# First expert block of 80 slots instead of 128, and two blocks behind branches instead of one

## The chip, the cores and the metric

The kernel runs on one core of a Trainium2 chip. A core has TensorE (PE) for matrix products, VectorE (DVE), ScalarE (ACT), GpSimd (POOL) and SyncE (SP, which issues the loads here); the engines run side by side and wait for each other by semaphores. The metric is the device time of one execution in microseconds; lower is better.

## What is computed

Two layers of a decoder on 256 tokens of width 1024, all in float32. Layer 0 ends in a dense feed-forward block, layer 1 in eight experts, of which each token uses the two with the highest router values:

```python
logits = jnp.dot(x2d, w_router)                    # (256, 8)
top_logits, top_e = lax.top_k(logits, TOP_K)       # two experts of each token
top_w = jax.nn.softmax(top_logits, axis=-1)
...
def expert_block(args):                            # rows of one expert, 1024 wide
    xb, e = args
    return (jax.nn.silu(xb @ w_gate[e]) * (xb @ w_up[e])) @ w_down[e]   # 1024 -> 3584 -> 1024
```

Each token's two results are added, weighted with `top_w`. 512 pairs of token and expert fall on eight experts, 64 on average; with the inputs of the reference the experts get 55, 69, 69, 67, 52, 63, 68 and 69 tokens.

## The kernel before, in words

Everything is written out by hand: no loop is left in the program, and the order on ScalarE and VectorE in the experts is the order of the code (`in_order`). Products are made in three passes of the type float32r: each operand x is split into a rounded part (`xh`) and the rest (`xl`), and `wh.xh + wl.xh + wh.xl` stands for `w.x`. The split of the weights is done by `split` (lines 101 and 102): ScalarE casts a half chunk of 128 x 1024, VectorE subtracts.

The stage of the experts (`moe`, `experts(0)`) goes like this:

- **Routing** (`moe_route`) finds for each token its place among the tokens of its expert (`pos`). `slots` holds the numbers 0 to 127 in every row.
- **Dispatch** (`dispatch`, for two experts at a time) makes a one-hot matrix `oh` of tokens by slots (line 1515), and 32 products (line 1529) gather the tokens of both experts: stationary is a 128-column slice of the tokens `uth` or `utl`, moving is `oh` with 2 x 128 columns. Result: `xh` and `xl`, 1024 on the partitions and slots along the free side. Four transposes of `oh` (line 1535) make `ot`, with which results are sent back.
- **Gate and up** (lines 1638 to 1640): for each expert and each of 7 parts of 512 hidden columns, 2 x 24 products. Stationary are 128 slots of `xh` or `xl`, moving are 512 columns of weights. `hidden` (lines 1252, 1253) makes silu(gate) x up, a tile of slots x 512.
- **Turn** (`turn`, line 1658): four transposes put the 512 hidden columns on the partitions (stationary 128 columns of `hid`, moving the identity), and ScalarE and VectorE split the result into `hh` and `hl` (lines 1661, 1662). It is issued `TURN` = 2 half chunks after `hidden`.
- **Down** (lines 1625 to 1627): 24 products with `hh` and `hl` as stationary and 512 moving weight columns, into two sums of slots x 512 that run over all 7 parts.
- **Bring** (`bring`, `add`, lines 1671 to 1680): the sums are split and sent back to the tokens by eight products with `ot`, and added to `h` with their weights.

Each expert's weights are 42 chunks of 1 MB. SP issues a load when the buffer before it has been read for the last time, which is by VectorE in line 102. TensorE's queue holds, for each expert, 7 x 72 products with 512 moving columns; between them lie the turns, the dispatch of the next pair of experts, and the way back.

Behind the stage stands a branch. `most` is the largest number of tokens of any expert; each engine loads it (line 1504) and jumps (line 1505) over a second copy of the whole block, for slots 128 to 255, which is not run with these inputs. Behind the jump the last stage begins (`ple`: transposes of `h` in line 150, products in lines 271 to 273, the output).

Of the kernel before, what the change touches and what calls it, by code (L numbers as in the profile page):

```python
# [10 lines left out]
F32 = mybir.dt.float32  # L11
F32R = mybir.dt.float32r
# [7 lines left out]
D = 1024  # L20
# [20 lines left out]

RATE = [[[0.9, 0.6, 1.04], [0.31, 0.22, 0.66], [0.3, 0.23, 0.38, 0.3, 0.3], [0.39, 0.25, 0.08, 0.12, 0.29], [2.4, 2.8, 2.8, 2.7], [1.4, 1.0, 0.8, 0.6], [1.0, 1.0, 1.0, 1.0, 1.0, 1.0], [0.0, 1.0, 1.0, 1.0]], [[0.55, 0.85, 1.15], [0.18, 0.12, 0.47], [0.3, 0.3, 0.3, 0.45, 0.3], [0.41, 0.71, 0.1, 0.0, 0.5], [2.7, 2.7, 2.7, 2.7], [0.5, 0.5, 0.5, 0.5], [1.0, 1.0, 1.0, 1.0, 1.0, 1.0], [0.0, 1.0, 1.0, 1.0]]]

LATE = 1
FROM = [6, 8]
WARM = 14, 8, 6
# [25 lines left out]
class Build:  # L72
# [363 lines left out]
    def mixer(self, l):  # L436
# [59 lines left out]
        def zchunks(a, b):  # L496
# [16 lines left out]
            for i, (c, fi) in enumerate(items):  # L513
# [8 lines left out]
                late.append((c, fi, ps))  # L522
                if len(late) > LATE:
                    finish(*late.pop(0))
# [720 lines left out]
                    finish(*late.pop(0))  # L1245
                yield

    def hidden(self, pg, pu, shape):

        nc = self.nc  # L1250
        hid = self.fx.tile(shape, F32, name="hid", tag="hid", bufs=2)
        nc.scalar.activation(hid, pg, AF.Silu)
        nc.vector.tensor_tensor(hid, pu, hid, op=OP.mult)
        return hid
# [245 lines left out]
    def moe(self):  # L1500
        nc, tc = self.nc, self.tc
        self.experts(0)
        if self.general:
            most = nc.values_load(self.cnti[0:1, 0:1], min_val=0, max_val=256)
            with tc.If(most > 128):
                self.experts(1)
        self.tap("hf1", self.h)

    def dispatch(self, e0, blk):

        nc, fx, M = self.nc, self.fx, self.M
        oh = fx.tile([128, 2, 256], F32R, name="oh", tag="oh", bufs=2)
        for tt in range(2):
            for i in range(2):
                nc.vector.tensor_scalar(oh[:, tt, i * 128:(i + 1) * 128], M["slots"], float(128 * blk),
                                        M["pos"][:, tt, e0 + i:e0 + i + 1], op0=OP.add, op1=OP.is_equal)
        yield
        xh = fx.tile([128, 8, 256], F32R, name="xh", tag="xh", bufs=2)
        xl = fx.tile([128, 8, 256], F32R, name="xl", tag="xl", bufs=2)
        ot = fx.tile([128, 2, 2, 128], F32R, name="ot", tag="ot", bufs=2)  # L1520
        self.X[e0 // 2] = xh, xl, ot
        sums = cycle([self.psm] if e0 else [self.psm, self.psz])
        for kp in range(4):
            for src, dst in ((M["uth"], xh), (M["utl"], xl)):
                ps = next(sums)(2, 256)
                for ki in range(2):
                    k = 2 * kp + ki
                    for tt in range(2):
                        nc.tensor.matmul(ps[:, ki], src[:, tt, k * 128:(k + 1) * 128], oh[:, tt], start=tt == 0, stop=tt == 1)
                nc.scalar.copy(dst[:, 2 * kp:2 * kp + 2], ps)  # L1530
                yield
        ps = self.psm(2, 2, 128)
        for i in range(2):
            for tt in range(2):
                nc.tensor.transpose(ps[:, i, tt], oh[:, tt, i * 128:(i + 1) * 128].bitcast(F32), self.ident)
        nc.scalar.copy(ot, ps)
        yield

    def halves(self):
# [21 lines left out]
    def experts(self, blk):  # L1561


        nc, A, fx = self.nc, self.A, self.fx
        mm = nc.tensor.matmul
        X, HID, HT, ACC, PS = self.X, {}, {}, {}, {}
        block = nc.cur_bb.bb

# [45 lines left out]
        def products(j):  # L1614
            w, e, n, i = halves[j]
            wh, wl = splits[j]
            splits[j] = None
            if w == "down":
                hh, hl = HT[e, n]
                if n == 0 and i == 0:  # L1620
                    ACC[e] = [self.psz(512) for _ in range(2)]
                for hf in range(2):
                    ws = slice(hf * 512, (hf + 1) * 512)
                    ps, f, z = ACC[e][hf], n == 0 and i == 0, n == 6 and i == 3
                    mm(ps, hh[:, i], wh[:, ws], start=f, stop=False)  # L1625
                    mm(ps, hh[:, i], wl[:, ws], start=False, stop=False)  # L1626
                    mm(ps, hl[:, i], wh[:, ws], start=False, stop=z)  # L1627
                if n == 6 and i == 3:
                    after(j, 0, lambda: bring(e))
                return  # L1630
            xh, xl, _ = X[e // 2]
            sl = slice((e % 2) * 128, (e % 2) * 128 + 128)
            if i == 0:
                PS[w] = self.psa(512)
            ps = PS[w]
            for ki in range(2):
                k, ws = 2 * i + ki, slice(ki * 512, (ki + 1) * 512)
                mm(ps, xh[:, k, sl], wh[:, ws], start=k == 0, stop=False)  # L1638
                mm(ps, xh[:, k, sl], wl[:, ws], start=False, stop=False)  # L1639
                mm(ps, xl[:, k, sl], wh[:, ws], start=False, stop=k == 7)  # L1640
            if w == "up" and i == 3:
                g, u = PS["gate"], PS["up"]
                after(j, 0, lambda: HID.update({(e, n): self.hidden(g, u, [128, 512])}))
                after(j, TURN, lambda: turn(e, n))
                if e % 2 and n == 1 and e < NE - 1:
                    st = self.dispatch(e + 1, blk)
                    for t in range(10):
                        after(j, 1 + t, lambda: next(st))

        def after(j, lag, fn):  # L1650
            due[j + lag].append(fn)

        def turn(e, n):

            hid = HID.pop((e, n))
            pt = self.psm(4, 128)
            for i in range(4):
                nc.tensor.transpose(pt[:, i], hid[:, i * 128:(i + 1) * 128], self.ident)
            hh = fx.tile([128, 4, 128], F32R, name="hh", tag="hh", bufs=2)
            hl = fx.tile([128, 4, 128], F32R, name="hl", tag="hl", bufs=2)  # L1660
            nc.scalar.copy(hh, pt)
            nc.vector.tensor_sub(hl, pt, hh.bitcast(F32))
            HT[e, n] = hh, hl

        def bring(e):

            acc, ot = ACC.pop(e), X[e // 2][2]
            yh, yl = (lambda t: (t[:, 0], t[:, 1]))(self.fy.tile([128, 2, D], F32R, name="yhl", tag="yhl"))
            for hf in range(2):
                ws = slice(hf * 512, (hf + 1) * 512)  # L1670
                nc.scalar.copy(yh[:, ws], acc[hf])
                nc.vector.tensor_sub(yl[:, ws], acc[hf], yh[:, ws].bitcast(F32))

            def add(tt, hf):
                ws = slice(hf * 512, (hf + 1) * 512)
                ps = self.psm(512)
                mm(ps, ot[:, e % 2, tt], yh[:, ws], start=True, stop=False)
                mm(ps, ot[:, e % 2, tt], yl[:, ws], start=False, stop=True)
# [15 lines left out]
        for j in range(len(due)):  # L1694
            at = j

            for _ in range((4, 2, 2, 0, 1)[j] if j < 5 else 0):
                next(st0)
            if j < len(halves):
                products(j)  # L1700
                split()
                if blk == 0 and j == EMBED - 24:
                    st = embed()
                    after(j, 0, lambda: next(st))
                    for t in range(7):
                        after(j, 24 - LEAD + t, lambda: next(st))
            for fn in due[j]:
                fn()
# [123 lines left out]
```

## Time and profile before

| | us |
|---|---|
| median of 3 runs | 1978.77 (1977.77 to 1978.91) |
| profiled execution | 1978.85 |
| its span, first to last instruction | 1977.1 |
| experts, first dispatch product to the last result added | 954 to 1942 |
| the last stage behind the branch | 1945 to 1977 |

TensorE is busy for 1926.7 us of the span (97%), VectorE for 1589.3 (80%), ScalarE for 1387.2 (70%). Products are pipelined: a record of TensorE runs from its start to a modelled end, so a record of 0.39 us may be followed by the next start after 0.23. What a product costs in a full queue is the distance of starts, and this is what is read below. In the rows a form such as `128*128 128x512` is the stationary operand (rows x columns) and the moving one. PEld is the load of the stationary operand, which overlaps with products. An engine's name with a q (PEldq, SPq) stands for its sequencer: jumps, semaphores, DMA issues.

### The profile page before, as it was taken

How to read it: one execution, taken by the hardware profiler on the slowest of the kernel's cores; microseconds unless marked ns; L12 is line 12 of the kernel's file. 1: busy time of each engine (PE TensorE's matmuls, PEld its weight loads, DVE VectorE, ACT ScalarE, POOL GpSimd, SP SyncE). 2: the span in 40 equal slices, each digit the busy share in tenths (PEclk: the TensorE clock that was granted, in tenths of full speed). 3: DMA queues.
4: the chain of work that ended last, by engine and by line, in shares of the span. 5: the costliest groups of instructions: out<-in, count | busy, mean ns of one | idle time of the engine just before them, and what ended most of it. 6: DMA issues, size and time to landing. Idle time of an engine off the chain costs nothing. (4 is left out here: it accounts for less than half of the span.)

```text
span 1977.1 us, 32507 instructions
## 1 busy us (share of the span) xinstructions
PE 1926.7 (97%) x12357; PEld 1640.6 (83%) x12357; DVE 1589.3 (80%) x2072; ACT 1387.2 (70%) x1981; POOL 13.8 (1%) x50
## 2 busy tenths in 40 slices
PE   8999999999999999999999999999999999999997
PEld 8878789899989868788888888888788888888886
DVE  6879757655576889466899899989899989999995
ACT  6776775644456686574787787878777777777773
POOL 1000000000000000000000000000000000000000
PEclk8999999999999999899999999999999999999999
DMA  5433225555534324048797899999899999999990
GB/s 208 138 115 129 87 103 191 194 191 189 186 129 157 114 97 152 24 155 313 266 365 299 328 373 362 373 368 350 315 361 377 374 333 368 357 383 372 357 360 29
DMA packets 92516, 491.38 MB, mean 249 GB/s; under 512 B 11168, under 2 KB 11424, under 8 KB 53184
## 3 DMA queue, kind: packets, MB, share of 16 engines
q1 hardware_dynamic: 89712, 485.04, 66.4%
q10 hardware_dynamic: 2640, 4.18, 0.7%
q8 instruction: 99, 1.62, 0.3%
q14 instruction: 65, 0.53, 0.1%
HBM read 488.13 MB, written 1.05 MB: 247 GB/s over the span
## 5 line engine op out<-in xcount | busy, mean ns | idle before, releaser
L102 DVE TENSOR_TENSOR wl<-rawm,wh 128x1024 fp32r<-128x1024 f32 x608 | 724.0, 1221 | 65.1 <-ACT wh L101 26.1
L101 ACT CAST wh<-rawm 128x1024 fp32r<-128x1024 f32 x608 | 628.9, 1054 | 117.2 <-PE ps_a L1640 72.8
L102 DVE TENSOR_TENSOR wl<-raw,wh 128x1024 fp32r<-128x1024 f32 x298 | 362.7, 1221 | 158.3 <-PE ps_z L109 89.3
L101 ACT CAST wh<-raw 128x1024 fp32r<-128x1024 f32 x298 | 312.3, 1050 | 132.1 <-PE ps_z L110 35.3
L108 PE MATMUL ps_z<-uh,wh 128*128 128x256 f32 x1232 | 358.9, 291 | 4.3 <-ACT wh L101 2.3
L110 PE MATMUL ps_z<-uh,wl 128*128 128x256 f32 x1232 | 352.3, 286 | 7.3 <-DVE wl L102 7.3
L109 PE MATMUL ps_z<-ul,wh 128*128 128x256 f32 x1232 | 350.1, 284 | 0.0
L1640 PE MATMUL ps_a<-wh,xl 128*128 128x512 f32 x896 | 349.8, 390 | 0.0
L1639 PE MATMUL ps_a<-wl,xh 128*128 128x512 f32 x896 | 349.5, 390 | 0.3 <-DVE wl L102 0.2
L1638 PE MATMUL ps_a<-wh,xh 128*128 128x512 f32 x896 | 349.5, 391 | 0.2 <-ACT wh L101 0.2
L108 PEld LDWEIGHTS ps_z<-uh,wh 128*128 128x128 f32 x1232 | 235.2, 191 | 16.2 <-issue 6.5
L110 PEld LDWEIGHTS ps_z<-uh,wl 128*128 128x128 f32 x1232 | 235.3, 191 | 14.7 <-DVE wl L102 10.7
L109 PEld LDWEIGHTS ps_z<-ul,wh 128*128 128x128 f32 x1232 | 235.2, 191 | 5.8 <-issue 4.4
L1639 PEld LDWEIGHTS ps_a<-wl,xh 128*128 128x128 f32 x896 | 168.3, 188 | 37.6 <-DVE wl L102 1.9
L1638 PEld LDWEIGHTS ps_a<-wh,xh 128*128 128x128 f32 x896 | 168.3, 188 | 35.8 <-ACT wh L101 0.9
L1640 PEld LDWEIGHTS ps_a<-wh,xl 128*128 128x128 f32 x896 | 168.2, 188 | 34.9 <-issue 0.5
L1627 PE MATMUL ps_z<-wh,hl 128*128 128x512 f32 x448 | 176.8, 395 | 0.0
L1626 PE MATMUL ps_z<-wl,hh 128*128 128x512 f32 x448 | 175.2, 391 | 0.4 <-DVE wl L102 0.4
L1625 PE MATMUL ps_z<-wh,hh 128*128 128x512 f32 x448 | 162.6, 397 | 0.2 <-ACT wh L101 0.2
L1626 PEld LDWEIGHTS ps_z<-wl,hh 128*128 128x128 f32 x448 | 84.2, 188 | 18.4 <-DVE wl L102 1.9
L1627 PEld LDWEIGHTS ps_z<-wh,hl 128*128 128x128 f32 x448 | 84.1, 188 | 17.2
L1625 PEld LDWEIGHTS ps_z<-wh,hh 128*128 128x128 f32 x448 | 84.2, 188 | 16.2 <-ACT wh L101 0.6
(556 smaller groups left out, 2433.2 us busy)
## 6 DMA issues: line engine op xcount, KB each, us to landing
rawm<-in_wmg_dram SPq DMA_DIRECT2D x199, 1024.0 KB, 6.6
rawm<-in_wmd_dram SPq DMA_DIRECT2D x101, 1024.0 KB, 6.7
raw<-in_wz_dram SPq DMA_DIRECT2D x112, 512.0 KB, 3.8
raw<-in_wmg_dram SPq DMA_DIRECT2D x50, 512.0 KB, 7.8
raw<-in_wff_dram SPq DMA_DIRECT2D x44, 512.0 KB, 4.1
raw<-in_wbr_dram SPq DMA_DIRECT2D x24, 512.0 KB, 4.7
raw<-in_wfd_dram SPq DMA_DIRECT2D x22, 512.0 KB, 3.7
raw<-in_wmd_dram SPq DMA_DIRECT2D x22, 512.0 KB, 8.0
```

Source lines behind the costliest of these rows:

```text
L101: nc.scalar.copy(h, raw)
L102: nc.vector.tensor_sub(l, raw, h.bitcast(F32))
L108: nc.tensor.matmul(ps, wh, xh, start=first, stop=False)
L109: nc.tensor.matmul(ps, wh, xl, start=False, stop=False)
L110: nc.tensor.matmul(ps, wl, xh, start=False, stop=last)
L1625: mm(ps, hh[:, i], wh[:, ws], start=f, stop=False)
L1626: mm(ps, hh[:, i], wl[:, ws], start=False, stop=False)
L1627: mm(ps, hl[:, i], wh[:, ws], start=False, stop=z)
L1638: mm(ps, xh[:, k, sl], wh[:, ws], start=k == 0, stop=False)
L1639: mm(ps, xh[:, k, sl], wl[:, ws], start=False, stop=False)
L1640: mm(ps, xl[:, k, sl], wh[:, ws], start=False, stop=k == 7)
```

## The change

The slots of an expert are covered by three blocks of 80, 128 and 48 slots instead of two of 128. The first is always run. The other two stand behind branches of their own, at more than 80 and at more than 208 tokens of the fullest expert; a branch follows the end of the other, they are not nested.

In the block every tile keeps its size and is used in part. `oh` has 2 x 80 columns, so the 32 products of a dispatch move 160 columns. `xh` and `xl` get an axis for the expert. The stationary operands of gate, up and down have 80 columns, sums and `hid` 80 partitions, and `turn` multiplies with an 80 x 80 corner of the identity.

```diff
+BLOCKS = ((0, 80), (80, 128), (208, 48))
...
-            with tc.If(most > 128):
-                self.experts(1)
+            for blk in range(1, len(BLOCKS)):
+                with tc.If(most > BLOCKS[blk][0]):
+                    self.experts(blk)
...
-        oh = fx.tile([128, 2, 256], F32R, name="oh", tag="oh", bufs=2)
+        start, cap = BLOCKS[blk]
+        oh = fx.tile([128, 2, 256], F32R, name="oh", tag="oh", bufs=2)[:, :, 0:2 * cap]
...
-                nc.vector.tensor_scalar(oh[:, tt, i * 128:(i + 1) * 128], M["slots"], float(128 * blk),
+                nc.vector.tensor_scalar(oh[:, tt, i * cap:(i + 1) * cap], M["slots"][:, 0:cap], float(start),
...
-        xh = fx.tile([128, 8, 256], F32R, name="xh", tag="xh", bufs=2)
+        xh = fx.tile([128, 8, 2, 128], F32R, name="xh", tag="xh", bufs=2)[:, :, :, 0:cap]
...
-                ps = next(sums)(2, 256)
+                ps = next(sums)(2, 2 * cap)
...
-                nc.scalar.copy(dst[:, 2 * kp:2 * kp + 2], ps)
+                nc.scalar.copy(dst[:, 2 * kp:2 * kp + 2], ps.rearrange("p k (e s) -> p k e s", e=2))
...
-                nc.tensor.transpose(ps[:, i, tt], oh[:, tt, i * 128:(i + 1) * 128].bitcast(F32), self.ident)
-        nc.scalar.copy(ot, ps)
+                nc.tensor.transpose(ps[0:cap, i, tt], oh[:, tt, i * cap:(i + 1) * cap].bitcast(F32), self.ident)
+        nc.scalar.copy(ot[0:cap], ps[0:cap])
...
-                    ACC[e] = [self.psz(512) for _ in range(2)]
+                    ACC[e] = [self.psz(512)[0:cap] for _ in range(2)]
...
-                mm(ps, xh[:, k, sl], wh[:, ws], start=k == 0, stop=False)
+                mm(ps, xh[:, k, e % 2], wh[:, ws], start=k == 0, stop=False)
...
-            pt = self.psm(4, 128)
+            pt = self.psm(4, cap)
             for i in range(4):
-                nc.tensor.transpose(pt[:, i], hid[:, i * 128:(i + 1) * 128], self.ident)
-            hh = fx.tile([128, 4, 128], F32R, name="hh", tag="hh", bufs=2)
+                nc.tensor.transpose(pt[:, i], hid[:, i * 128:(i + 1) * 128], self.ident[0:cap, 0:cap])
+            hh = fx.tile([128, 4, 128], F32R, name="hh", tag="hh", bufs=2)[:, :, 0:cap]
...
-                mm(ps, ot[:, e % 2, tt], yh[:, ws], start=True, stop=False)
+                mm(ps, ot[0:cap, e % 2, tt], yh[:, ws], start=True, stop=False)
```

The program has the same instructions in the part that is run, in nearly the same order. On TensorE, at the start of the block, the order before has the five small products of the routing, six that only keep the engine at work (line 145), and the first dispatch, whose last number is the shape of the result:

```order
L1468 MATMUL ps_m<-msel,onr 128x8
L145 MATMUL ps_z<-ones 128x128 x6
L1529 MATMUL ps_m<-oh,uth 128x256
L1529 MATMUL ps_z<-oh,utl 128x256 x2
L1529 MATMUL ps_m<-oh,uth 128x256 x3
L1529 MATMUL ps_z<-oh,utl 128x256 x6
```

The same place of the change:

```order
L1533 MATMUL ps_m<-oh,uth 128x160
L1533 MATMUL ps_z<-oh,utl 128x160
L1533 MATMUL ps_m<-oh,uth 128x160 x3
L1533 MATMUL ps_z<-oh,utl 128x160 x5
L1533 MATMUL ps_m<-oh,uth 128x160 x4
```

The results have 160 columns instead of 256, and one product of the second sum has moved behind three of the first.

On TensorE at the end of the block, with the last result sent back, the load of `cnti` (the largest count), the jump, the first rows of the block that it passes over, and behind the dots what follows that block, before:

```order
L1678 MATMUL ps_m<-yhl,ot 128x512
L1504 TENSOR_LOAD cnti
L1505 COMPARE_AND_BRANCH
L1529 MATMUL ps_m<-oh,uth 128x256 x4
...
L1505 UNCONDITIONAL_BRANCH x2
L150 MATMUL ps_m<-ident,h 128x128 x8
```

And in the change:

```order
L1682 MATMUL ps_m<-yhl,ot 128x512
L1506 TENSOR_LOAD cnti
L1508 COMPARE_AND_BRANCH
L1533 MATMUL ps_m<-oh,uth 128x256 x4
...
L1508 UNCONDITIONAL_BRANCH x2
L1508 COMPARE_AND_BRANCH
L1533 MATMUL ps_m<-oh,uth 128x96 x4
...
L1508 UNCONDITIONAL_BRANCH x2
L152 MATMUL ps_m<-ident,h 128x128 x8
```

The end of the first passed block is now followed by a second jump over a second block of as many rows, with 2 x 48 columns in its dispatches, and only then by the transposes of the last stage.

## Rows read from the trace of the kernel before

**Rows 1.** Busy time of each engine in the experts' stage, granted clock, DMA.

```profile
core 0: us, PE busy (x) PEld busy (x) DVE busy (x) ACT busy (x) POOL busy (x), PEclk, DMA share, GB/s
1000.00:1900.00 900.00, 899.14 (x4088) 739.87 (x4087) 822.91 (x787) 707.02 (x773) 0.00 (x0) 1.00 0.94 357
```

**Rows 2.** Waits from 1000 to 1900 us (total, times, longest), VectorE for loads.

```profile
DVE wl L102 <- DMA rawm<-in_wmg_dram: 2.0, 3, 1.4
```

**Rows 3.** Waits of SyncE's DMA queue in the same stretch.

```profile
SPq L88 <- DVE wl L102: 725.0, 270, 6.3
```

**Rows 4.** TensorE in order of time, experts: start us, us, line, form.

```profile
1079.43 0.39 PE L1639 MATMUL ps_a<-wl,xh 128*128 128x512 f32 x1
...
1080.80 0.39 PE L1639 MATMUL ps_a<-wl,xh 128*128 128x512 f32 x1
```

**Rows 5.** TensorE in order of time, layer 1's mixer: 128, then 64 stationary columns.

```profile
635.39 0.28 PE L108 MATMUL ps_z<-uh,wh 128*128 128x256 f32 x1
...
636.10 0.28 PE L108 MATMUL ps_m<-uh,k2a 128*64 128x256 f32 x1
...
636.93 0.28 PE L109 MATMUL ps_m<-ul,k2a 128*64 128x256 f32 x1
```

**Rows 6.** TensorE in order of time, layer 1's output projection.

```profile
929.89 0.40 PE L273 MATMUL ps_a<-wh,ul 128*128 128x512 f32 x1
...
931.29 0.40 PE L273 MATMUL ps_a<-wh,ul 128*128 128x512 f32 x1
```

**Rows 7.** TensorE in order of time around one turn.

```profile
1085.10 0.39 PE L1627 MATMUL ps_z<-wh,hl 128*128 128x512 f32 x1
1085.33 0.60 PE L1658 MATMUL ps_m<-ident,hid 128*128 128x128 f32 x4
...
1086.00 0.40 PE L1626 MATMUL ps_z<-wl,hh 128*128 128x512 f32 x1
```

**Rows 8.** Three lines with plain f32: duration ns min/median/max, first and last start.

```profile
L1155 PE MATMUL ps_m<-cv x32: 377/379/634, 202.3 to 845.3; 96*128 96x256 f32 x32
...
L1658 PE MATMUL ps_m<-ident,hid x224: 270/272/273, 973.9 to 1929.5; 128*128 128x128 f32 x112
...
L695 PE MATMUL ps_m<-ident,t x48: 216/222/273, 84.1 to 696.3; 64*128 64x64 f32 x48
```

**Rows 9.** TensorE in order of time in the first dispatch.

```profile
959.99 0.64 PE L1529 MATMUL ps_m<-oh,uth 128*128 128x256 f32 x4
...
960.94 0.40 PE L1638 MATMUL ps_a<-wh,xh 128*128 128x512 f32 x1
```

**Rows 10.** TensorE in order of time in the routing.

```profile
951.96 0.24 PE L1464 MATMUL ps_m<-msel,ltr 128*128 128x8 f32 x1 [0.25 <-ACT wh L101]
...
952.40 0.25 PE L1468 MATMUL ps_m<-msel,onr 128*128 128x8 f32 x1
```

**Rows 11.** Groups of ScalarE by form: busy us, mean ns, idle before.

```profile
L1252 ACT ACTIVATE hid<-ps_a 128x512 f32<-128x512 f32 x56 | 33.0, 589 | 0.0
...
L1252 ACT ACTIVATE hid<-ps_z 128x256 f32<-128x256 f32 x22 | 8.5, 385 | 32.7 <-PE ps_z L110 32.7
```

**Rows 12.** Line 1505, the jump: duration ns min/median/max, first and last start.

```profile
L1505 ACTq COMPARE_BRANCH  x1: 50/50/50, 1938.2 to 1938.2; - x1
L1505 ACTq EVENT_SEMAPHORE  x1: 17/17/17, 1940.8 to 1940.8; - x1
L1505 PEldq COMPARE_BRANCH  x1: 3746/3746/3746, 1941.3 to 1941.3; - x1
L1505 DVEq COMPARE_BRANCH  x1: 72/72/72, 1942.1 to 1942.1; - x1
L1505 DVEq EVENT_SEMAPHORE  x1: 21/21/21, 1945.1 to 1945.1; - x1
```

**Rows 13.** TensorE in order of time around the jump.

```profile
1940.55 0.40 PE L1678 MATMUL ps_m<-yhl,ot 128*128 128x512 f32 x1
1945.40 1.94 PE L150 MATMUL ps_m<-ident,h 128*128 128x128 f32 x8 [4.45 <-PEq L1505]
```

**Rows 14.** Busy times behind the jump, columns as in rows 1.

```profile
1945.50:1950.50 5.00, 5.00 (x20) 4.66 (x21) 3.48 (x5) 4.04 (x6) 0.00 (x0) 0.50 0.02 5
```

More of the change, by code (lines that the diff above doesn't have):

```diff
@@ L1246, in merge, with hidden @@
                 yield
-    def hidden(self, pg, pu, shape):
+    def hidden(self, pg, pu, shape, rows=128):
         nc = self.nc
-        hid = self.fx.tile(shape, F32, name="hid", tag="hid", bufs=2)
+        hid = self.fx.tile(shape, F32, name="hid", tag="hid", bufs=2)[0:rows]
         nc.scalar.activation(hid, pg, AF.Silu)
@@ L1511, in dispatch @@
         nc, fx, M = self.nc, self.fx, self.M
-        oh = fx.tile([128, 2, 256], F32R, name="oh", tag="oh", bufs=2)
+        start, cap = BLOCKS[blk]
+        oh = fx.tile([128, 2, 256], F32R, name="oh", tag="oh", bufs=2)[:, :, 0:2 * cap]
         for tt in range(2):
             for i in range(2):
-                nc.vector.tensor_scalar(oh[:, tt, i * 128:(i + 1) * 128], M["slots"], float(128 * blk),
+                nc.vector.tensor_scalar(oh[:, tt, i * cap:(i + 1) * cap], M["slots"][:, 0:cap], float(start),
                                         M["pos"][:, tt, e0 + i:e0 + i + 1], op0=OP.add, op1=OP.is_equal)
         yield
-        xh = fx.tile([128, 8, 256], F32R, name="xh", tag="xh", bufs=2)
-        xl = fx.tile([128, 8, 256], F32R, name="xl", tag="xl", bufs=2)
+        xh = fx.tile([128, 8, 2, 128], F32R, name="xh", tag="xh", bufs=2)[:, :, :, 0:cap]
+        xl = fx.tile([128, 8, 2, 128], F32R, name="xl", tag="xl", bufs=2)[:, :, :, 0:cap]
         ot = fx.tile([128, 2, 2, 128], F32R, name="ot", tag="ot", bufs=2)
@@ L1565, in experts @@
         mm = nc.tensor.matmul
+        cap = BLOCKS[blk][1]
         X, HID, HT, ACC, PS = self.X, {}, {}, {}, {}
@@ L1631, in products @@
             xh, xl, _ = X[e // 2]
-            sl = slice((e % 2) * 128, (e % 2) * 128 + 128)
             if i == 0:
-                PS[w] = self.psa(512)
+                PS[w] = self.psa(512)[0:cap]
             ps = PS[w]
@@ L1637, in products @@
                 k, ws = 2 * i + ki, slice(ki * 512, (ki + 1) * 512)
-                mm(ps, xh[:, k, sl], wh[:, ws], start=k == 0, stop=False)
-                mm(ps, xh[:, k, sl], wl[:, ws], start=False, stop=False)
-                mm(ps, xl[:, k, sl], wh[:, ws], start=False, stop=k == 7)
+                mm(ps, xh[:, k, e % 2], wh[:, ws], start=k == 0, stop=False)
+                mm(ps, xh[:, k, e % 2], wl[:, ws], start=False, stop=False)
+                mm(ps, xl[:, k, e % 2], wh[:, ws], start=False, stop=k == 7)
             if w == "up" and i == 3:
                 g, u = PS["gate"], PS["up"]
-                after(j, 0, lambda: HID.update({(e, n): self.hidden(g, u, [128, 512])}))
+                after(j, 0, lambda: HID.update({(e, n): self.hidden(g, u, [128, 512], cap)}))
                 after(j, TURN, lambda: turn(e, n))
@@ L1655, in turn @@
             hid = HID.pop((e, n))
-            pt = self.psm(4, 128)
+            pt = self.psm(4, cap)
             for i in range(4):
-                nc.tensor.transpose(pt[:, i], hid[:, i * 128:(i + 1) * 128], self.ident)
-            hh = fx.tile([128, 4, 128], F32R, name="hh", tag="hh", bufs=2)
-            hl = fx.tile([128, 4, 128], F32R, name="hl", tag="hl", bufs=2)
+                nc.tensor.transpose(pt[:, i], hid[:, i * 128:(i + 1) * 128], self.ident[0:cap, 0:cap])
+            hh = fx.tile([128, 4, 128], F32R, name="hh", tag="hh", bufs=2)[:, :, 0:cap]
+            hl = fx.tile([128, 4, 128], F32R, name="hl", tag="hl", bufs=2)[:, :, 0:cap]
             nc.scalar.copy(hh, pt)
@@ L1667, in bring @@
             acc, ot = ACC.pop(e), X[e // 2][2]
-            yh, yl = (lambda t: (t[:, 0], t[:, 1]))(self.fy.tile([128, 2, D], F32R, name="yhl", tag="yhl"))
+            yh, yl = (lambda t: (t[0:cap, 0], t[0:cap, 1]))(self.fy.tile([128, 2, D], F32R, name="yhl", tag="yhl"))
             for hf in range(2):
@@ L1676, in add @@
                 ps = self.psm(512)
-                mm(ps, ot[:, e % 2, tt], yh[:, ws], start=True, stop=False)
-                mm(ps, ot[:, e % 2, tt], yl[:, ws], start=False, stop=True)
+                mm(ps, ot[0:cap, e % 2, tt], yh[:, ws], start=True, stop=False)
+                mm(ps, ot[0:cap, e % 2, tt], yl[:, ws], start=False, stop=True)
                 nc.vector.scalar_tensor_tensor(self.h[:, tt, ws], ps, self.M["wt"][:, tt, e:e + 1], self.h[:, tt, ws],
```

## The prediction, made before the changed kernel was run

> **What bounds the kernel now.** I read first the table of busy times by stretch, then the waits, then the order in time on TensorE, then the instructions of single lines. The experts run from 954 to 1941 us, half of the span. In the 900 us from 1000 to 1900 TensorE is busy for 899.14 us at granted clock 1.00; VectorE is busy for 822.91, ScalarE for 707.02, and the DMA engines are 94% busy [rows 1]. So TensorE sets the pace. The DMA does not: VectorE waits for weights 3 times and 2.0 us in all [rows 2], while the queue that issues the loads waits 270 times and 725.0 us for VectorE to give a buffer back [rows 3]. Whatever shortens TensorE's queue in this stage shortens the kernel, and what ACT and DVE save there is worth nothing by itself.
>
> What fills that queue is 8 experts x 7 parts x 72 = 4032 products with 512 moving columns. They follow each other at (1080.80 - 1079.43) / 6 = 0.228 us [rows 4], some 920 of the 987 us. The rest is 56 turns of four transposes, four dispatches of 32 products and four transposes, the way back of the sums and 16 products of the embedding.
>
> **The products: nothing.** The change makes the stationary operand 80 columns wide instead of 128 (in the products and in the sums' return, where it cuts the contraction to 80 rows, it leaves the 512 moving columns). The nearest rows: a run whose stationary operand falls from 128 to 64 columns, with 256 moving. Before, (636.10 - 635.39) / 6 = 0.118 us a product; after, (636.93 - 636.10) / 7 = 0.119 [rows 5]. So a narrower stationary operand buys no time, and I take 0 x 4032. The bounds are what a digit of these rows can hide, 1 ns either way, hence -4.0 to +4.0 us. Lines 1252, 1253, 1671 and 1672 have 80 partitions and as many elements in each; they cost the same.
>
> **The turns: -9.0 us.** Each of the 224 transposes of `hid` now moves 80 columns of `ident` instead of 128. Four of them lie between a product that starts at 1085.10 and the second one after them at 1086.00: 0.90 us where two products alone would take 0.455. So a turn costs 0.445 us of queue, 0.111 a transpose [rows 7]. How that goes with the columns: a plain f32 product takes 379 ns at 256 columns, a transpose 272 at 128 and 222 at 64 [rows 8], that is 0.84 and 0.78 ns a column. I take 0.83: 48 columns fewer give 40 ns, 224 x 40 ns = 9.0 us. The other end is the price of a one-pass column, (0.228 - 0.119) / 256 = 0.43 ns, from [rows 4, 5]: 20 ns a transpose, 4.6 us. I take the upper one because the rows nearest to it are transposes.
>
> The Trainium skill bears on this term: "TensorE: Matmul & The Clock Gate", section Back-to-back issue gap, gives N / 2.4 + 2.5 ns between matmuls at full clock, 55.8 ns for 128 columns and 35.8 for 80. The row shows 0.111 us at 128, twice that; the measurement decides; by the page's difference of 20 ns the sum would be an estimate of 1977.0.
>
> **The dispatches: -1.1 us.** 128 products (line 1529) move 160 columns of `oh` instead of 256. Eight of them now take 960.94 - 959.99 = 0.95 us, 0.119 each [rows 9]. By the 0.43 ns a column they would come to 0.078, but the stationary side, a slice of `uth` or `utl`, keeps 128 columns, and that has a floor: five products of the same type with 8 moving columns follow each other at (952.40 - 951.96) / 4 = 0.110 us [rows 10]. So 9 ns each, 128 x 9 ns = 1.1 us. No row shows this type between 8 and 256 columns. If it ran there at the f32 price, 160 x 0.84 = 0.134 us, each would cost 15 ns more than now, +1.9 us; the range takes both. The 16 transposes of `oh` still move 128 columns of `ident`: 0.
>
> **ScalarE and VectorE: nothing on the path.** The copies and subtractions of the turns (56 each) and the 32 copies of the dispatches shrink from 512 to 320 elements. An activation takes 589 ns at 512 and 385 at 256 [rows 11], 0.8 ns an element, so some 0.15 us each and 13 us of ScalarE in all. TensorE's own work covers that: the transposes are issued two half chunks after `hidden`, and the rows on TensorE show it busy all the time. If the cover were gone it would be a gain of a few tenths at the start of the stage. I take 0.
>
> **The second branch: +3.8 us.** Line 1505 is a compare and jump on every engine over a block of some 4,000 TensorE rows that is not run. On TensorE the record of it lasts 3746 ns, from 1941.3, and the first work behind it starts at 1945.40, 4.85 us after the last product [rows 12, 13]. The other engines' records are 50 to 72 ns, but their next instruction comes 2.6 us later on ScalarE (1938.2 to 1940.8) and 3.0 on VectorE (1942.1 to 1945.1): all pay a like stall. In the changed order a second compare and jump stands right behind the first one's end, with another block of that size behind it, so TensorE jumps twice in a row. What is queued behind it on TensorE are the transposes of `h` for the last stage, for which ScalarE and VectorE wait there; nothing can be pulled ahead. Bounds: 2.6 us (ScalarE's gap) to 4.45 us (TensorE's whole idle time there); I take the record itself and 0.05 for the join. The clock is low behind the jump anyway: it is 0.50 from 1945.5 to 1950.5 [rows 14], the lower of the two levels (1.2 GHz), after the idle time. A longer pause cannot lower it further, and I take that stretch as unchanged.
>
> Two pages of the Trainium skill differ on this. "Advanced Engine Details and Errata", Control Flow Timing, gives about 108 ns for a compare and branch; "Runtime: NRT & Kernel Launch", Instruction fetch mechanics, says that a taken branch to a target outside the fetched window waits until the target has been fetched by DMA. The record of 3746 ns agrees with the second; by the first the second branch would cost 0.1 and the sum would be an estimate of 1968.8.
>
> **The sum.** The profiled execution took 1978.85 us, 1.75 more than its span of 1977.1, and the median of the three runs is 1978.77, so the two bases agree within 0.1. -9.0 - 1.1 + 3.8 = -6.3, and 1978.8 - 6.3 = 1972.5, 0.32% below. With the products' 4.0 us either way and 2.6 to 4.45 for the branch this case alone lies between 1967.3 and 1977.2.
>
> **Rivals.** All but the first are this sum with one term replaced.
>
> *The products stretch (slower).* Products of one shape do not cost the same everywhere: in the output projection, same 128 x 128 and 512 columns, they follow at (931.29 - 929.89) / 6 = 0.233 us, 6 ns above the experts' [rows 6]. Something other than the shape, the place of the operands I think, moves the step. Rows of 80 in a tile laid out for 128 move every operand's place. At 6 ns, 4032 x 6 = +24 us: 1996.7. It turns the sign at 6.3 / 4032 = 1.6 ns and is slower by more than 4.0 us from 2.6 ns on. Against it: the run with 64 columns [rows 5] shows no more than 1 ns. Chance 0.12.
>
> *The transposes have a fixed share*, and only 0.43 ns a column falls away: -4.6 instead of -9.0, 1976.9. For it: each still loads 128 columns of `hid`, and the page's formula above gives the same difference. Against: the 64-column row [rows 8]. Chance 0.12.
>
> *The dispatch products lose their one-pass price below 256 columns*: +1.9 instead of -1.1, 1975.5. Nothing in the trace speaks for or against. Chance 0.12.
>
> *Another engine takes over.* With TensorE 1% faster, VectorE at 91% and the DMA at 94% could become last, the gain goes and the branch stays: 1978.8 + 3.8 = 1982.6. For it: only a few per cent of room. Against: [rows 2, 3], and VectorE has less to do too. Chance 0.07.
>
> *The second jump is nearly free*, because its target is already under way: 1978.8 - 10.1 + 0.1 = 1968.8. Chance 0.04.
>
> *The change does not do what it says*: an expert with more than 80 tokens would run the whole second block, another 983 us as the first takes: some 2956. The reference's inputs give the experts 55, 69, 69, 67, 52, 63, 68 and 69 tokens, 11 below. Chance 0.01.
>
> **How the numbers follow.** The forecast has 0.47, the rivals 0.48, and 0.05 is left for what I have not thought of. A measurement of this kernel tells 0.2% from no change, 4.0 us: below 1974.8 is faster, above 1982.7 slower. Faster: most of the forecast (0.41), a little of the dispatch and transpose rivals (0.05), the free jump (0.04): 0.50. Slower: the stretch, half of the engine that takes over, the block that runs, and a share of the unknown: 0.17. Same: 0.33. The range from 1967 to 1983 takes in all but the stretch from 3 ns on and the block.
>
> **What would show it.** Right: line 1658's transposes at about 234 ns and starts 0.07 us apart; the products still 0.228 apart; the 160-column products 0.110 apart; two records of some 3.7 us for the branches on TensorE and the last stage starting about 8.6 us after the last product. Wrong: products at 0.230 or more, transposes still 0.1 apart, 160-column products at 0.13 or more, TensorE waiting for VectorE or for a load in the middle of the stage, or one long branch record and a short one.

## The result and the profile after

The changed kernel takes 1997.04 us (median of 4 runs, 1995.38 to 1998.32), the kernel before 1978.82 beside it: ratio 1.0097 [1.0085, 1.0109], **slower by 18 us**, where I forecast 6 us faster. It came out as the rival "the products stretch" had it (1996.7).

Its profiled execution has a span of 1993.7 us, 16.6 more than before. From the first dispatch product to the last product of the block (956.44 to 1953.26 us; before 953.96 to 1940.55) it takes 996.8 us instead of 986.6: +10.2. The gap behind the block grew by 4.5, the part behind the gap is 0.6 shorter, and 2.5 us lie ahead of the block, in code that nothing here touches. That start lies between 950.9 and 957.9 in the twelve traces of this study, so I count those 2.5 us as scatter. The terms that the trace shows, 10.2 + 4.5 - 0.6 = 14.1 us, are most of the 18.2 between the two medians; the rest is these 2.5 us and the 1.7 by which the profiled execution lies below its kernel's median, and no term of the change is shown in it.

First the table of busy times in the same 900 us as [rows 1], with the same columns:

```profile
1000.00:1900.00 900.00, 898.78 (x4042) 580.20 (x4041) 808.44 (x778) 690.25 (x765) 0.00 (x0) 1.00 0.94 353
```

TensorE is as full as before and at the same clock, VectorE and ScalarE have less to do. Yet the count of TensorE's records fell from 4088 to 4042: it gets through less work in the same full time (some records are missing in any trace, so the steps below are the better measure). PEld, the loads of stationary operands, fell from 740 to 580 us, and the queue as a whole is no faster for it.

The waits that answer to [rows 2, 3]: VectorE for loads, and the queue that issues the loads for VectorE.

```profile
DVE wl L104 <- DMA raw<-in_wmg_dram: 0.6, 1, 0.6
...
SPq L90 <- DVE wl L104: 716.2, 264, 6.1
```

No other engine took over: VectorE hardly waits for loads, and loads still wait for buffers. TensorE's own products are slower. Two starts, 24 products apart, against the 0.228 of [rows 4]:

```profile
1201.06 0.39 PE L1644 MATMUL ps_a<-wh,xl 128*80 128x512 f32 x1
...
1206.66 0.39 PE L1644 MATMUL ps_a<-wh,xl 128*80 128x512 f32 x1
```

5.60 us for 24 is 0.2333 each. Over all pairs of neighbouring products in the trace (starts less than 260 ns apart) the mean step went from 227.3 to 233.2 ns in gate and up and from 228.3 to 232.7 in down: 2688 x 5.9 + 1344 x 4.4 = **+21.8 us**.

The turns, as in [rows 7], then the transposes as in [rows 8] (duration ns min/median/max), then a dispatch of eight products as in [rows 9]:

```profile
1088.63 0.40 PE L1632 MATMUL ps_z<-wh,hl 128*80 128x512 f32 x1
1088.87 0.44 PE L1662 MATMUL ps_m<-ident,hid 80*128 80x80 f32 x4
...
1089.38 0.39 PE L1631 MATMUL ps_z<-wl,hh 128*80 128x512 f32 x1
```

```profile
L1662 PE MATMUL ps_m<-ident,hid x224: 230/232/235, 976.1 to 1942.1; 80*128 80x80 f32 x112
```

```profile
959.91 0.57 PE L1533 MATMUL ps_m<-oh,uth 128*128 128x160 f32 x4
...
960.76 0.40 PE L1642 MATMUL ps_a<-wh,xh 128*80 128x512 f32 x1
```

A turn with its two products takes 0.75 us instead of 0.90 (medians over the 56: 0.744 and 0.9005); less two products of each kernel's own step that is 0.277 instead of 0.445, or **-9.4 us** in 56 turns. Eight dispatch products take 0.85 us instead of 0.95, so 0.106 each: 128 x 0.013 = **-1.6 us**. What the turns' gain consists of, `turn80` shows below. 21.8 - 9.4 - 1.6 = +10.8, beside +10.2 measured for the block.

Last the branch: the records of the two jumps (as in [rows 12]), then the products around them (as in [rows 13]), then the stretch behind with its clock (as in [rows 14]).

```profile
L1508 ACTq COMPARE_BRANCH  x2: 45/48/50, 1950.9 to 1953.5; - x2
...
L1508 PEldq COMPARE_BRANCH  x2: 3479/4016/4552, 1954.0 to 1957.7; - x2
L1508 DVEq COMPARE_BRANCH  x2: 56/64/72, 1954.8 to 1957.7; - x2
```

```profile
1953.26 0.40 PE L1682 MATMUL ps_m<-yhl,ot 80*128 80x512 f32 x1
1962.59 1.94 PE L152 MATMUL ps_m<-ident,h 128*128 128x128 f32 x8 [8.94 <-PEq L1508]
```

```profile
1962.70:1967.70 5.00, 5.00 (x25) 4.68 (x26) 3.48 (x5) 4.27 (x7) 0.00 (x0) 0.73 0.02 3
```

Two records, 3479 and 4552 ns, and 9.33 us between the last product and the next stage instead of 4.85: **+4.5 us**. The stretch behind is at 0.73 here, a mix of the two levels, where it was at 0.50: the granted clock, which fell in the gap, is back at the upper level 2.8 us after the last stage's first product, where it took 5.4 before. That is the 0.6 us by which this part is shorter. It is no gain of the change: in `two_branches`, with the same two jumps, the clock comes back only after 6.1 us and the part is 0.9 longer.

### The profile page after: what moved, and what is told of

It is laid out like the page before. It is cut to its first block, busy times and chain, and to the rows that moved or that the text cites. A ratio compares the mean times of both kernels' runs of the same rounds, so it can differ in the third digit from the quotient of the medians.

```text
span 1993.7 us, 32523 instructions
## 1 busy us (share of the span) xinstructions
PE 1937.0 (97%) x12357; PEld 1473.8 (74%) x12357; DVE 1581.9 (79%) x2072; ACT 1374.9 (69%) x1981; POOL 13.8 (1%) x50
## 5 line engine op out<-in xcount | busy, mean ns | idle before, releaser
L1642 PE MATMUL ps_a<-wh,xh 128*80 128x512 f32 x896 | 355.2, 397 | 0.3 <-ACT wh L103 0.3
L1643 PE MATMUL ps_a<-wl,xh 128*80 128x512 f32 x896 | 354.6, 396 | 0.0
L1644 PE MATMUL ps_a<-wh,xl 128*80 128x512 f32 x896 | 354.4, 396 | 0.0
L1643 PEld LDWEIGHTS ps_a<-wl,xh 128*80 128x80 f32 x896 | 132.6, 148 | 76.4 <-DVE wl L104 2.4
L1644 PEld LDWEIGHTS ps_a<-wh,xl 128*80 128x80 f32 x896 | 132.5, 148 | 75.3
L1642 PEld LDWEIGHTS ps_a<-wh,xh 128*80 128x80 f32 x896 | 132.7, 148 | 75.0 <-ACT wh L103 1.9
L1632 PE MATMUL ps_z<-wh,hl 128*80 128x512 f32 x448 | 177.5, 396 | 0.0
L1631 PE MATMUL ps_z<-wl,hh 128*80 128x512 f32 x448 | 176.7, 395 | 0.6 <-DVE wl L104 0.6
L1630 PE MATMUL ps_z<-wh,hh 128*80 128x512 f32 x448 | 164.3, 398 | 0.4 <-ACT wh L103 0.4
L1631 PEld LDWEIGHTS ps_z<-wl,hh 128*80 128x80 f32 x448 | 66.4, 148 | 35.4 <-DVE wl L104 0.9
```

The source lines that it names most:

```text
L1642: mm(ps, xh[:, k, e % 2], wh[:, ws], start=k == 0, stop=False)
L1643: mm(ps, xh[:, k, e % 2], wl[:, ws], start=False, stop=False)
L1644: mm(ps, xl[:, k, e % 2], wh[:, ws], start=False, stop=k == 7)
```

## The experiments

All numbers of a block below are from the first dispatch product to the block's last product, and steps are means over neighbouring products, both as above. A run without an interval was executed once.

### The branch alone, and the branch nested

`two_branches` is the change with a first block of 128 slots, so that only the second branch is left of it:

```diff
-BLOCKS = ((0, 80), (80, 128), (208, 48))
+BLOCKS = ((0, 128), (128, 80), (208, 48))
```

> The changed kernel with blocks of 128, 80 and 48 slots: the first block is as in the kernel before, and the second branch is added alone. By the record of the changed kernel (4.55 and 3.48 us on TensorE, the gap up from 4.85 to 9.34) it costs 4.5 us: ratio 1.0023. If the second branch cost nothing by itself and the gap were a matter of the block's narrow operands: 1.0000.

Measured: 1986.47 us, ratio 1.0039 [1.0026, 1.0051]. The block takes 986.7 us, as before, with steps of 227.3 and 228.3 ns. The products around the jumps:

```profile
1940.63 0.40 PE L1682 MATMUL ps_m<-yhl,ot 128*128 128x512 f32 x1
1950.04 1.94 PE L152 MATMUL ps_m<-ident,h 128*128 128x128 f32 x8 [9.01 <-PEq L1508]
```

The gap is 9.41 us, +4.6. So the second branch costs its 4.5 us without anything else of the change. The ratio's interval is +5 to +10 us: the gap is a little below its lower end, and the part behind the gap is 0.9 us longer here; what lies above I have not traced.

`nested` is the change with the third block inside the branch of the second, so that one jump passes over both:

```diff
-            for blk in range(1, len(BLOCKS)):
-                with tc.If(most > BLOCKS[blk][0]):
-                    self.experts(blk)
+            with tc.If(most > BLOCKS[1][0]):
+                self.experts(1)
+                with tc.If(most > BLOCKS[2][0]):
+                    self.experts(2)
```

> The changed kernel with its third block's branch put inside the second block, so that one jump is taken and not two. If the second jump is what the gap of 9.34 us holds above 4.85: 4.5 us below the changed kernel's 1997.0, 1992.5, ratio to before 1.007. If a jump over two blocks costs as much as two jumps: 1997, 1.009.

Measured: 1990.83 us, ratio 1.0056 [1.0035, 1.0077], where the change has 1.0097.

```profile
1952.88 0.40 PE L1683 MATMUL ps_m<-yhl,ot 80*128 80x512 f32 x1
1957.90 1.51 PE L152 MATMUL ps_m<-ident,h 128*128 128x128 f32 x6 [4.61 <-PEq L1507]
```

5.02 us of gap: the jump over twice as much code costs what one jump cost before (4.85). The block takes 996.9 us, with 233.3 and 232.7 ns a product, as in the change. So the branch's 4.5 us are the price of two jumps in a row, and they can be had back; the products' cost stays and is the larger one.

### What stretches the products: the width?

`w1` and `w2` are the kernel before (its layout, its dispatch, its one branch) with another width of the stationary operands for each expert. The edit, with the widths of `w1`; `w2` has 127, 120, 104, 100, 88, 84, 81, 72. In `w1` the experts with fewer slots than tokens leave tokens out.

```diff
+W = (128, 96, 64, 32, 112, 80, 48, 16)
...
-            sl = slice((e % 2) * 128, (e % 2) * 128 + 128)
+            sl = slice((e % 2) * 128, (e % 2) * 128 + W[e])
...
-            pt = self.psm(4, 128)
+            pt = self.psm(4, cap)
```

> The kernel before, with one thing altered by expert: the stationary operands of gate, up and down (and with them hid, the turn's identity and the way back) are 128, 96, 64, 32, 112, 80, 48 and 16 columns wide for experts 0 to 7. Dispatch and branch are those of before. Experts with fewer columns than tokens leave the rest of their tokens out. Read: the mean distance of starts of the products of each expert. Theory A, a step is longer whenever the operand is narrower than 128: 227.6 ns in expert 0, 231 to 235 in all others. Theory B, it is longer where the width is not a multiple of 32: 227.6 in experts 0 to 3, 231 to 235 at 112, 80, 48 and 16. Theory C, the width has nothing to do with it (another part of the change does it): 227 to 229 everywhere, 80 included.

> As the run before it, with widths 127, 120, 104, 100, 88, 84, 81 and 72 for experts 0 to 7. Theory A: all at 231 to 235 ns, or growing as the width falls. Theory B: all at 231 to 235, with no order in the width. Theory C: 227 to 229 everywhere. A fourth, D, that the step follows the moment at which the load of the operand ends (0.83 ns a column): then it changes smoothly between neighbours, 84, 81 and 80 of the two runs within 1 ns of each other.

Measured: 1994.57 and 1989.88 us. Pairs of starts 24 products apart, first `w1` with 128, 96 and 80 columns, then `w2` with 84 and 81:

```profile
987.03 0.39 PE L1639 MATMUL ps_a<-wh,xh 128*128 128x512 f32 x1
...
992.48 0.39 PE L1639 MATMUL ps_a<-wh,xh 128*128 128x512 f32 x1
...
1127.92 0.39 PE L1639 MATMUL ps_a<-wh,xh 128*96 128x512 f32 x1
...
1133.44 0.39 PE L1639 MATMUL ps_a<-wh,xh 128*96 128x512 f32 x1
...
1577.53 0.40 PE L1639 MATMUL ps_a<-wh,xh 128*80 128x512 f32 x1
...
1583.13 0.40 PE L1639 MATMUL ps_a<-wh,xh 128*80 128x512 f32 x1
```

```profile
1578.12 0.39 PE L1640 MATMUL ps_a<-wl,xh 128*84 128x512 f32 x1
...
1583.62 0.39 PE L1640 MATMUL ps_a<-wl,xh 128*84 128x512 f32 x1
...
1701.75 0.40 PE L1639 MATMUL ps_a<-wh,xh 128*81 128x512 f32 x1
...
1707.35 0.40 PE L1639 MATMUL ps_a<-wh,xh 128*81 128x512 f32 x1
```

24 products take 5.45 us at 128 columns, 5.52 at 96 and 64, 5.60 at 80 and 81, 5.50 at 84. The mean steps of gate and up in ns, by width: 128: 227.4; 127: 233.2; 120: 233.2; 112: 229.1; 104: 229.2; 100: 233.4; 96: 230.1; 88: 231.0; 84: 229.3; 81: 233.1; 80: 233.0; 72: 230.4; 64: 230.1; 48: 233.5; 32: 231.9; 16: 230.5. So 15 narrower widths all cost more than 128, by 1.7 to 6.1 ns, in no order: one column off 128 costs as much as 48 off. Nothing of the changed layout is needed for it. Theory C is out, and so are B, which spares multiples of 32, a price that spares multiples of 16, and one that grows as the operand shrinks. D is out as well: 84 and 81 columns differ by 3.8 ns. A is right that every narrower operand costs, but its 231 to 235 ns hold for 8 of the 15 widths; the others lie between 229.1 and 230.5. That the expert or its place in the program does it is out too: 80 columns cost 233.0 here in expert 5 alone, and 233.1 to 233.4 in each of the change's eight experts.

`cap96` takes one width of that list through the whole changed kernel:

```diff
-BLOCKS = ((0, 80), (80, 128), (208, 48))
+BLOCKS = ((0, 96), (96, 112), (208, 48))
```

> The changed kernel with blocks of 96, 112 and 48 slots. Theory W: products at 230.1 ns as those of 96 columns in the run with eight widths, +9.5 us; transposes of 96 columns -6.0, dispatches of 192 columns -1.0, two jumps one behind the other +4.5: +7.0 us, ratio 1.0035, 11 us faster than the change. Rival (any width under 128 costs about the same in a whole kernel): products at 233, +22 us as in the change, ratio 1.010.

Measured: 1984.34 us, ratio 1.0042 [1.0027, 1.0057], steps of 230.1 ns in gate and up and 230.0 in down. The list's value for 96 holds in a whole kernel, and the kernel with *more* slots beats the change.

### Or the place?

`place` has operands of 80, 80, 80, 96, 64, 64, 96 and 128 columns, and gate and up take them from columns 0, 48, 16, 0, 0, 64, 32 and 0 on; tokens in other slots are left out.

```diff
-            sl = slice((e % 2) * 128, (e % 2) * 128 + 128)
+            sl = slice((e % 2) * 128 + START[e], (e % 2) * 128 + START[e] + W[e])
```

> The kernel before with stationary operands of 80, 80, 80, 96, 64, 64, 96 and 128 columns for experts 0 to 7, of which gate and up take the slots from 0, 48, 16, 0, 0, 64, 32 and 0 on (tokens in other slots are left out of the result). Rival P (the place of the operand, my guess before the run): the step of gate and up changes with the start, by more than 1 ns between equal widths. Theory W (the width sets it, in no order): 233.0 ns for all three of 80, 230.1 for both of 96 and both of 64, 227.4 for the last. Rival E (it belongs to the expert or to its place in the program, not to the width): expert 0 as before near 227.4, expert 7 near 230.5, expert 3 near 231.7. Time by W: +14 for the products, -8 for the turns, +6 us in all, some 1985.

Measured: 1992.23 us. Steps of gate and up: 80 columns from 0 on 233.1, from 48 on 230.2, from 16 on 230.1; 96 columns from 0 on 230.2, from 32 on 231.6; 64 columns 230.0 and 229.9; 128 columns 227.7. Down of the two experts with shifted slots, whose operands still begin at column 0, steps by 232.4 and 232.6. The 80 columns from 48 and from 16 on:

```profile
1149.11 0.40 PE L1640 MATMUL ps_a<-wh,xh 128*80 128x512 f32 x1
...
1154.60 0.39 PE L1640 MATMUL ps_a<-wh,xh 128*80 128x512 f32 x1
...
1201.01 0.39 PE L1640 MATMUL ps_a<-wh,xh 128*80 128x512 f32 x1
...
1206.53 0.39 PE L1640 MATMUL ps_a<-wh,xh 128*80 128x512 f32 x1
```

5.49 and 5.52 us where 80 columns from 0 on take 5.60. At equal width the start moves the step by up to 3.0 ns, so the theory that width alone sets it fell. (The time is 7 us above what I expected. Dear turns of 64 rows make some 4 of them, see the last section; the rest I have not traced.)

That left full operands. `packed80` is the change with the odd experts' slots 80 columns, not 128, behind the even ones':

```diff
-        xh = fx.tile([128, 8, 2, 128], F32R, name="xh", tag="xh", bufs=2)[:, :, :, 0:cap]
+        xh = fx.tile([128, 8, 256], F32R, name="xh", tag="xh", bufs=2)[:, :, 0:2 * cap].rearrange("p k (e s) -> p k e s", e=2)
```

> The changed kernel with the slots of two experts packed: the stationary operands of odd experts start 80 columns behind those of the even ones and no longer 128. Theory P: gate and up of the odd experts leave 233.2 ns, as the 80 columns from 16 and from 48 on did (230), while the even experts stay: up to 1344 x 3 = 4 us less than the change. Theory W: 233.2 for all experts, time as the change.

Measured: 1988.93 us, the block 993.1 instead of 996.8. Gate and up step by 233.0 to 233.3 ns in the even experts and 230.1 to 230.5 in the odd ones. An even expert, then an odd one, 24 products each:

```profile
1450.66 0.39 PE L1642 MATMUL ps_a<-wh,xh 128*80 128x512 f32 x1
...
1456.27 0.39 PE L1642 MATMUL ps_a<-wh,xh 128*80 128x512 f32 x1
...
1572.00 0.39 PE L1642 MATMUL ps_a<-wh,xh 128*80 128x512 f32 x1
...
1577.52 0.39 PE L1642 MATMUL ps_a<-wh,xh 128*80 128x512 f32 x1
```

`pad132` is the kernel before with operands still 128 wide, but 132 columns from one to the next:

```diff
-        xh = fx.tile([128, 8, 256], F32R, name="xh", tag="xh", bufs=2)
+        xh = fx.tile([128, 8, 2, 132], F32R, name="xh", tag="xh", bufs=2)[:, :, :, 0:128]
```

> The kernel before, with xh and xl laid out as 8 x 2 x 132 columns instead of 8 x 256, of which 128 are used: the stationary operands of gate and up stay 128 wide, but their starts now step by 528 bytes, so that the 16 of them have 16 different places within 512 bytes. Down is as before. Theory P (the place moves the step of a full operand too, which would explain the 0.233 of the output projection, rows 6): some of the 16 places at 229 to 233 ns, the mean of gate and up at 228.5 or more, 3 to 16 us. Theory W (the place matters for narrower operands alone): 227.3 at all places, time as before.

Measured: 1994.65 us, the kernel before 1979.21 beside it. Gate and up step by 231.5 to 232.3 ns in all eight experts: (231.9 - 227.3) x 2688 = 12.4 us, and the block grew by 12.5. Two starts 24 products apart:

```profile
1460.68 0.39 PE L1638 MATMUL ps_a<-wh,xh 128*128 128x512 f32 x1
...
1466.24 0.39 PE L1638 MATMUL ps_a<-wh,xh 128*128 128x512 f32 x1
```

That is 5.56 us. The steps differ by k: the three products of one k take some 686 to 704 ns, where the kernel before has 680 in its undisturbed stretches. This is a loss of the change's size with nothing made narrower.

`shift` moves all operands of a pair of experts together and leaves their distances alone:

```diff
+SHIFT = (4, 16, 32, 64)
...
-        xh = fx.tile([128, 8, 256], F32R, name="xh", tag="xh", bufs=2)
+        xh = fx.tile([128, 2112], F32R, name="xh", tag="xh", bufs=2)[:, SHIFT[e0 // 2]:SHIFT[e0 // 2] + 2048].rearrange("p (k s) -> p k s", k=8)
```

> The kernel before, with stationary operands of gate and up still 128 wide and 1024 bytes from one k to the next, but all of them moved together: by 16 bytes for experts 0 and 1, 64 for 2 and 3, 128 for 4 and 5, 256 for 6 and 7 (xh and xl lie in tiles that are 64 columns longer). Theory A (what counts is where an operand lies, not how it lies to the one before it): gate and up at 229 ns or more for some of the four shifts, up to 16 us in all. Theory N (only a change of place from one operand to the next costs, as in the layout with 132 columns): 227.3 at all four, time as before. In the first case the two experts of a pair agree, since they lie 512 bytes apart.

Measured: 1984.8 us, the kernel before 1977.64 beside it; the block takes 994.7 us, +8.1. Starts 24 products apart at 16, 64, 128 and 256 bytes:

```profile
985.35 0.39 PE L1639 MATMUL ps_a<-wh,xh 128*128 128x512 f32 x1
...
990.79 0.39 PE L1639 MATMUL ps_a<-wh,xh 128*128 128x512 f32 x1
...
1229.58 0.40 PE L1639 MATMUL ps_a<-wh,xh 128*128 128x512 f32 x1
...
1235.18 0.40 PE L1639 MATMUL ps_a<-wh,xh 128*128 128x512 f32 x1
...
1665.16 0.40 PE L1639 MATMUL ps_a<-wh,xh 128*128 128x512 f32 x1
...
1670.74 0.39 PE L1639 MATMUL ps_a<-wh,xh 128*128 128x512 f32 x1
...
1819.86 0.40 PE L1639 MATMUL ps_a<-wh,xh 128*128 128x512 f32 x1
...
1825.31 0.39 PE L1639 MATMUL ps_a<-wh,xh 128*128 128x512 f32 x1
```

5.44, 5.60, 5.58 and 5.45 us. Means: 227.3 and 227.5 ns at 16 bytes, 233.4 and 233.3 at 64, 232.8 and 232.3 at 128, 227.5 and 227.1 at 256 (the kernel before: 226.7 to 228.1 in its eight experts); the two experts of a pair agree. So where a full operand lies moves the step by 6 ns, with every distance between operands as before. Together with the widths: the step depends on *which* bytes of a partition a stationary operand takes up, by its start and by its width; how many they are does not settle it (128 columns cost 227 or 233 ns, 80 cost 230 or 233). Why, and by which rule, stays open; I have no rule that gives these values. One rival is left for the width: a narrower operand also gives a result of fewer rows, and no run separates that from the bytes at which the operand ends. It can't be the whole cause, since operands of one width differ.

### Keeping the gain without the cost

`turn80` leaves products and dispatches 128 wide, shortens the turns alone to 80 slots, and nests the blocks behind. The turns write columns 0 to 79 of `hh` and `hl`, whose other columns were set to zero once.

```diff
-                nc.tensor.transpose(pt[:, i], hid[:, i * 128:(i + 1) * 128], self.ident)
+                nc.tensor.transpose(pt[:, i], hid[0:cap, i * 128:(i + 1) * 128], self.ident[0:cap, 0:cap])
...
-            nc.scalar.copy(hh, pt)
+            nc.scalar.copy(hh[:, :, 0:cap], pt)
```

> The kernel before, with its products and dispatches left as they are (stationary operands of 128 columns), but with turns of 80 slots: the transposes move an 80 x 80 corner of the identity and write columns 0 to 79 of two pairs of hh and hl, whose other columns were set to zero once. The blocks behind start at 80 and 208, and the third stands inside the second's branch, so that one jump passes over both. Theory W (the 22 us are the price of stationary operands narrower than 128 columns, and nothing else in the changed block costs): products 227.3 and 228.3 ns apart as before, transposes 69 ns apart, one gap of 5.0 us at the end: -9.0 + 0.2 = -8.8 us, ratio 0.9955. Rival T (the shorter turns, or what ScalarE and VectorE do around them, upset the queue of products): products at 229 ns or more here too; from 2.2 ns on the gain is gone, at 5.5 ns the ratio is 1.007.

Measured: **1971.89 us, ratio 0.9965 [0.9954, 0.9977]**, faster than both kernels. First 24 products, then a turn, then the end of the block:

```profile
1201.19 0.39 PE L1649 MATMUL ps_a<-wh,xl 128*128 128x512 f32 x1
...
1206.63 0.39 PE L1649 MATMUL ps_a<-wh,xl 128*128 128x512 f32 x1
```

```profile
1087.67 0.39 PE L1636 MATMUL ps_z<-wh,hl 128*128 128x512 f32 x1
1087.90 0.44 PE L1667 MATMUL ps_m<-ident,hid 80*128 80x80 f32 x4
...
1088.46 0.39 PE L1635 MATMUL ps_z<-wl,hh 128*128 128x512 f32 x1
```

```profile
1936.01 0.40 PE L1686 MATMUL ps_m<-yhl,ot 128*128 128x512 f32 x1
1940.83 1.51 PE L151 MATMUL ps_m<-ident,h 128*128 128x128 f32 x6 [4.42 <-DVEq L1506]
```

Products are back at 5.44 us for 24 (mean 227.1), the gap is 4.82 us, and the block takes 978.5 us, -8.1. A turn with its two products takes 0.784 us (median): 56 x (0.9005 - 0.784) = -6.5, less than the -9.0 expected. Between the four transposes lie three steps, and each shrank by 39 ns (108 to 69 or 70), here as in the change: that is the whole 0.117 us. In the change another 0.041 us falls away behind the turn, where its second product starts 0.275 us after its first, not 0.316 as here and before. The load of that second product's stationary operand takes 188 ns with 128 columns and 148 with 80, and in `w2` the same step falls with the load, from 0.315 us (load 187 ns) at 127 columns to 0.269 (142 ns) at 72. So the load is not hidden at this one place. Of the remaining -1.6 us some 0.9 are mean steps 0.2 ns shorter in all 4032 products, less than the experts of one trace differ among themselves; the rest I have not traced.

## Why the prediction was wrong, point by point

- **The products: 0 predicted, bounds 4.0 us either way; +21.8 measured.** This is the step that failed. I took a run with 256 moving columns, in another stage, with operands in other places [rows 5], for the experts' products, and put the bound at "what a digit of these rows can hide, 1 ns". The row showed 0.118 against 0.119 and was true there; it could not speak for operands that lie elsewhere. Even its bound was too narrow: starts are given to 0.01 us, so 0.71 / 6 and 0.83 / 7 are uncertain by up to 1.7 and 1.4 ns. Against a count of 4032 every ns is 4 us.
- **The rival that came true** had the right size and half of the reason. [rows 6] showed products of the same shape at 0.233, and I guessed the place of the operands. That the place can do this to a full operand is shown (`shift`: the same 5.60 us for 24); whether it is what stretches the products of [rows 6] no run tests. But the change moves no start: the operands begin at the same columns of xh and hh as before. What it changes is the width, and with it the end, and that costs as much (`w1`, `w2`). So that the rival's 1996.7 us lie beside the measured 1997.04 is partly luck: its 6 ns came from another stage, and 96 columns would have cost 2.8 ns (`cap96`). With a row in hand that showed 6 ns, an unknown cost of that size belonged in the products' bounds.
- **The turns: -9.0 predicted, -9.4 measured** in the change. The price of 0.83 ns a column holds for a transpose: durations 272 to 232 ns, starts 108 to 70 ns apart. The transposes' fixed share did not come true. But that the whole turn came out right is in part luck: I counted 40 ns for each of four transposes, the starts show it three times a turn, or -6.5 us (`turn80`), and a term that I had at nothing, the shorter load of the stationary operand behind the turn, gave 56 x 0.041 = 2.3 us more. (The remaining 0.6 of the 9.4 comes of taking off two products at each kernel's own step.)
- **The dispatches: -1.1 predicted, -1.6 measured** (0.106 a product where I took 0.110).
- **The second branch: +3.8 predicted, +4.5 measured**, a hair above the upper bound of 4.45. Two records in a row, as forecast; the second was the longer one.
- **The stretch behind the branch: 0 predicted, -0.6 measured**, which goes with the granted clock, as said above, and not with the change.
- **ScalarE and VectorE: 0 predicted, nothing seen.** No other engine took over.
- By this sum with the products at +21.8, the time would have been 1978.8 + 21.8 - 9.0 - 1.1 + 3.8 = 1994.3, beside 1997.04 measured; for the remaining 2.7 us no term of the change is traced.

## What to carry to other kernels

Before narrowing the stationary operand of a full TensorE queue, find every row of the same moving width in the trace and compare their steps: where two rows of one shape differ, something outside the shape sets the step, and the sum needs a term of at least that difference, times the count. Here fewer columns pay where they *move* (the transposes, 0.8 ns each). Columns that are only loaded were hidden already, but for the load right behind a turn, and cutting them cost 1.7 to 6.1 ns a product. Put blocks that are hardly ever run behind one jump, nested, not one jump each.

## What the runs showed of the hardware that I had not expected

- **Start and width of the stationary operand move the step of a product of 512 columns between 226.7 and 233.5 ns** in these rows. Three products take 680 ns for the kernel before, 690 for 96 columns, 700 for 80, for 81 and for a full operand moved by 64 bytes. The load of 80 columns takes 148 ns, that of 128 took 188 (medians), and in 98% or more of the products of gate and up it ends before its product starts; the shorter one left the next product later. The Trainium skill, "TensorE: Matmul & The Clock Gate", section Step-by-step: what each phase is for, says that loading the next operand does not take read bandwidth from the running product, since the two have ports of their own. By that the place should make no difference to a load that is hidden; `shift` shows that it does, 64 bytes for 6 ns.
- **Turns of 64 rows or fewer are dearer than turns of 128.** From `w1`, with 64 slots:

```profile
1228.12 0.39 PE L1628 MATMUL ps_z<-wh,hl 128*64 128x512 f32 x1
1228.44 0.46 PE L1659 MATMUL ps_m<-ident,hid 64*128 64x64 f32 x4
...
1229.12 0.39 PE L1627 MATMUL ps_z<-wl,hh 128*64 128x512 f32 x1
```

  1.00 us where 128 rows take 0.90 and 80 rows 0.75: the first transpose starts 0.32 us behind the product, not 0.23, and the way back takes longer too. With 48, 32 and 16 rows it is 0.97, 0.95 and 0.92 (medians of 7). A first block of 64 slots would have lost the turns' gain as well.
- **Two jumps in a row add up** (gaps of 9.33 to 9.89 us in four kernels, against 4.85), and one jump over two blocks costs hardly more than over one (5.02 in `nested`, 4.82 in `turn80`). The Trainium skill, "Runtime: NRT & Kernel Launch", section Instruction fetch mechanics, says that a taken branch out of the fetched window waits for a DMA to fetch its target; the number of jumps, and not their length, setting the price agrees with it.
